# Forgetting attention: the mask products of two token blocks, one behind the other

## The chip, the cores and the metric

The kernel runs on one core of a Trainium2 chip. The metric is the device time of one launch in microseconds, the median over runs. The core has a matrix engine (TensorE, PE in the profile; its weight loads are the rows PEld), a vector engine (VectorE, DVE), a scalar engine (ScalarE, ACT), GpSimd (POOL) and SyncE (SP), which issues the DMAs. Each engine works through its own instructions in program order and waits for the others by semaphores.

## What is computed

A trunk of two decoder layers over 512 tokens of 1024 channels, in float32. Each layer is a SwiGLU half step, a token mixer and a second SwiGLU half step, with RMS norms around each. The mixer of the second layer is forgetting attention with 16 heads of 64 channels, and the change lies there:

```python
def _fox_attention(q, k, v, zf, b_f):
    logf = jax.nn.log_sigmoid(zf.astype(jnp.float32) + b_f.astype(jnp.float32))
    c = jnp.cumsum(logf.transpose(0, 2, 1), axis=-1)
    ...
        sc = jnp.einsum("bhqd,bhkd->bhqk", qs, kh).astype(jnp.float32) / math.sqrt(dh)
        sc = sc + cs[..., :, None] - c[..., None, :]
        sc = jnp.where(tpos[:, None] >= key_pos[None, :], sc, NEG)
        p = jax.nn.softmax(sc, axis=-1)
        return jnp.einsum("bhqk,bhkd->bhqd", p.astype(vh.dtype), vh)
```

## The kernel before

A float32 matrix product is made of three products of rounded parts (type float32r): each operand is split into a high part, rounded by ScalarE (`split`, line 69), and a low part, the rest, by VectorE; `mm3` (lines 74 to 76) adds high x high, high x low and low x high in one PSUM bank. The tile framework places the instructions: it takes the program, and with a timing model of its own it puts each engine's instructions into an order. So code that stands together is not together on an engine unless the data or a declared dependency makes it so.

`odd` (from line 599) is the mixer of the second layer. Per head, `project` computes the queries and keys (24 products of 512 columns), and `put_qk` empties that bank into four tiles QA, KA, QC, KC (lines 620 to 627), of which there are two sets, for even and odd heads. `project_v` computes the values of four heads for one block of 128 tokens (24 products of 256 columns).

`scores(h)` is where the change lies. The 512 query tokens of a head are four blocks b of 128, and block b sees (b + 1) x 128 keys. Its scores are a sum of three products in PSUM: line 688 (QA and KA, which also carry the gates), line 689 (the low parts), and line 690, the mask: a bf16 identity times a bf16 triangle of zeros and -1e30, added to the last 128 columns of the block. Then VectorE takes the maximum over the keys (692), ScalarE the exponential and its sum (693), VectorE the reciprocal (694) and the scaling (695). The scores of a head take three of four PSUM banks of the pool `acc`: blocks 0 and 1 share one, block 2 and block 3 have one each. A product into a bank waits until the exponentials that read it are done.

`transposed` turns the probabilities, ten blocks of 128 x 128 a head (line 710), into banks of the pool `mm`, and splits them; `values` multiplies them with the values (line 720, eight products). The loop calls scores(h + 1) ahead of transposed(h), so that a head's softmax runs beside the projections and the values of the head before. Heads are counted from 0.

Of the kernel before, what the change touches and what calls it, by code (L numbers as in the profile page):

```python
# [7 lines left out]


# [2 lines left out]

# [9 lines left out]
AF = mybir.ActivationFunctionType  # L22
ALU = mybir.AluOpType
AX = mybir.AxisListType
PSUM = bass.MemoryType.PSUM

P = 128
S = 512
NT = S // P
# [11 lines left out]
class Kernel:  # L41
# [145 lines left out]
    def turn_half(self, t, h, xg, which):  # L187
        nc = self.nc
        tp = self.psum(which)
        for k in range(4):  # L190
            nc.tensor.transpose(tp[:, k * P : (k + 1) * P], xg[:, k * P : (k + 1) * P], self.ident)
        ks, toks = slice(4 * h, 4 * h + 4), slice(t * P, (t + 1) * P)
        self.turned = self.split(self.hT[0][:, ks, toks], self.hT[1][:, ks, toks],
                                 tp.rearrange("p (k c) -> p k c", c=P))


    def ffn(self, l, s, norms, nxt, held=None):
# [401 lines left out]
    def odd(self, l, i, nxt):  # L599
        nc, tc, a = self.nc, self.tc, self.a  # L600
        w_qk, w_v0, w_v, w_out = (a["fox_w_" + n][i] for n in ("qk", "v0", "v", "out"))
        H = 16
        with ExitStack() as ctx:
# [10 lines left out]
            QA, KA, QC, KC = ([pc.tile([P, S], F32R, name=f"{n}{m}") for m in range(2)]  # L614
                              for n in ("qa", "ka", "qc", "kc"))
# [60 lines left out]
            def scores(h):  # L676
                m = h % 2
                banks = [self.psum("acc") for _ in range(3)]
                outs = [banks[0][:, 0:P], banks[0][:, P : 3 * P], banks[1][:, : 3 * P], banks[2]]
                pes = [self.wk() for _ in range(3)]  # L680
                pr = [pes[0][:, 0:P], pes[0][:, P : 3 * P], pes[1][:, : 3 * P], pes[2]]
                nm = self.small.tile([P, NT], F32, name="fnm")
                sm = self.small.tile([P, NT], F32, name="fsm")
                for b in range(NT):
                    n = (b + 1) * P
                    toks = slice(b * P, n)
                    ps = outs[b]
                    nc.tensor.matmul(ps, QA[m][:, toks], KA[m][:, :n], start=True, stop=False)  # L688
                    nc.tensor.matmul(ps, QC[m][:, toks], KC[m][:, :n], start=False, stop=False)
                    nc.tensor.matmul(ps[:, b * P : n], self.ident16, self.tri, start=False, stop=True)  # L690
                    bs = slice(b, b + 1)
                    nc.vector.tensor_reduce(nm[:, bs], ps, AX.X, ALU.max, negate=True)
                    nc.scalar.activation(pr[b], ps, AF.Exp, bias=nm[:, bs], accum_out=sm[:, bs])
                    nc.vector.reciprocal(sm[:, bs], sm[:, bs])
                    nc.vector.tensor_scalar(pr[b], pr[b], sm[:, bs], None, ALU.mult)
                return pr

            half = {}
# [63 lines left out]
            for h, (o, u) in enumerate(zip(pqk, u01)):  # L762
                self.proj(o[:, 256:], u, slice(256, 512))
                put_qk(h, o)
            project_v(1, 0)
            pr = scores(0)
            for h in range(H):
                pr2 = scores(h + 1) if h + 1 < H else None
                if h == 0:
                    project(h + 2)  # L770
                at = transposed(pr)
                if 0 < h < H - 2:
                    project(h + 2)
                if h >= 12:
                    early(h - 12)
                elif h >= 4:
                    project_v(h // 4 + 1, h % 4)
                elif h < 3:
                    project_v(1, 1 + h)
                values(h, at)  # L780
                pr = pr2
# [6 lines left out]
            for t in range(NT):  # L788
                toks = slice(t * P, (t + 1) * P)
# [160 lines left out]
```

## Time and profile before

| | us |
|---|---|
| median of 3 runs | 1948.91 (1948.52 to 1951.02) |
| the profiled execution | 1946.51 |
| its span | 1944.7 |
| TensorE busy in the span | 1911.6 |
| mask products (line 690), 64 of them, busy | 14.7 |

The span runs from the first to the last instruction of one profiled execution; the launch around it makes the difference to its time. Busy time of TensorE counts overlapping products once. [...] Attention of the second layer lies between 1340 and 1580 us.

### The profile page before, as it was taken

The page shows a single profiled execution, that of the slowest core. Times are in us where ns is not written, and L with a number is a line of the kernel's source. Part 1 is how long each engine was busy: PE and PEld are TensorE (multiplying, and loading weights), DVE is VectorE, ACT ScalarE, POOL GpSimd, SP SyncE. Part 2 cuts the span into 40 slices and gives each one's busy share as a digit, 9 for nine tenths or more (in the row PEclk, how much of TensorE's full clock was granted, in tenths as well). Part 3 has the DMA queues.
Part 4 walks back from the last instruction along what each step waited for, and adds up shares of the span by engine and source line. Part 5 has one row for each costly group of instructions (what it writes and reads, how often), then busy time and mean ns, then how long its engine had stood idle before and what let it go on. Part 6 is the DMA issues. An engine that isn't in the chain of part 4 may idle for free.

```text
span 1944.7 us, 24019 instructions
## 1 busy us (share of the span) xinstructions
PE 1911.6 (98%) x9715; PEld 1624.2 (84%) x9715; DVE 941.9 (48%) x1355; ACT 722.9 (37%) x1245; POOL 187.3 (10%) x250
## 2 busy tenths in 40 slices
PE   9999999999999999999999999999999999999998
PEld 8888888988788888888988888898888888888887
DVE  6333333589764333343633333356667563333333
ACT  6322221435654222222532222246666553222221
POOL 1000000333230000000200000014331110000000
PEclk9999999999999999999999999999999999999999
DMA  6323232131024323221442323222121323232311
GB/s 205 121 88 107 87 130 76 44 100 65 22 98 152 103 92 100 96 98 33 142 130 87 107 88 102 73 67 66 66 65 56 109 86 123 93 101 90 106 55 44
DMA packets 51265, 178.39 MB, mean 92 GB/s; under 512 B 7346, under 2 KB 7346, under 8 KB 51154
## 3 DMA queue, kind: packets, MB, share of 16 engines
q1 hardware_dynamic: 51154, 176.86, 28.1%
q8 instruction: 76, 1.25, 0.3%
q14 instruction: 35, 0.29, 0.1%
HBM read 174.74 MB, written 2.10 MB: 91 GB/s over the span
## 4 chain that ended last, share of the span: by engine, by line
PE 52%; issue 39%; DVE 3%; ACT 3%; POOL 2%; DMA 1%; POOLq 0%; DVEq 0%; SPq 0%; ACTq 0%
PE mm L74 14%; PE mm L75 14%; PE mm L76 14%; PE acc L74 2%; PE acc L75 2%; PE acc L76 2%; PE mm L710 1%; ACT whi L69 1%; POOL rstd L136 1%; PE mm L720 1%; POOL ms L134 1%; DMA raw<-in_ffn_w_up_dram 1%; ACT junk L141 1%; PE acc L688 0%; POOL wlo L69 0%
## 5 line engine op out<-in xcount | busy, mean ns | idle before, releaser
L74 PE MATMUL mm<-hhi,whi 128*128 128x512 f32 (+1 forms) x1952 | 693.6, 357 | 8.4 <-ACT hhi L69 7.8
L75 PE MATMUL mm<-hlo,whi 128*128 128x512 f32 (+1 forms) x1952 | 695.6, 357 | 2.7 <-DVE hlo L69 2.4
L76 PE MATMUL mm<-hhi,wlo 128*128 128x512 f32 (+1 forms) x1952 | 695.4, 357 | 0.0
L69 ACT CAST whi<-raw 128x1024 fp32r<-128x1024 f32 x319 | 331.3, 1050 | 894.7 <-issue 259.9
L69 DVE TENSOR_TENSOR wlo<-raw,whi 128x1024 fp32r<-128x1024 f32 (+1 forms) x293 | 355.0, 1226 | 370.3 <-ACT whi L69 355.9
L74 PEld LDWEIGHTS mm<-hhi,whi 128*128 128x128 f32 x1952 | 368.0, 189 | 62.9 <-ACT hhi L69 9.7
L75 PEld LDWEIGHTS mm<-hlo,whi 128*128 128x128 f32 x1952 | 369.6, 189 | 56.0 <-DVE hlo L69 4.1
L76 PEld LDWEIGHTS mm<-hhi,wlo 128*128 128x128 f32 x1952 | 369.6, 189 | 52.3
L215 DVE TENSOR_TENSOR wk<-mm,wk 128x512 f32<-128x512 f32 (+1 forms) x96 | 62.1, 647 | 291.6 <-PE mm L76 246.2
L252 DVE TENSOR_TENSOR ysb<-mm,ysb 128x512 f32<-128x512 f32 x128 | 88.5, 691 | 161.4 <-PE mm L76 161.4
L134 POOL TENSOR_SCALAR ms<-ss 128x1 f32<-128x1 f32 x48 | 24.0, 501 | 1463.1 <-ACT junk L141 1461.6
L76 PE MATMUL mm<-whi,alo 128*128 128x512 f32 x352 | 137.1, 389 | 0.0
L75 PE MATMUL mm<-wlo,ahi 128*128 128x512 f32 x352 | 137.0, 389 | 0.0
L76 PE MATMUL acc<-whi,alo 128*128 128x512 f32 x352 | 136.9, 389 | 0.0
L74 PE MATMUL acc<-whi,ahi 128*128 128x512 f32 x352 | 136.9, 389 | 0.0
L75 PE MATMUL acc<-wlo,ahi 128*128 128x512 f32 x352 | 136.9, 389 | 0.0
L74 PE MATMUL mm<-whi,ahi 128*128 128x512 f32 x352 | 136.8, 390 | 0.0
L214 ACT ACTIVATE wk<-mm 128x512 f32<-128x512 f32 (+1 forms) x96 | 53.0, 552 | 69.7 <-PE mm L76 69.7
L76 PEld LDWEIGHTS mm<-whi,alo 128*128 128x128 f32 x352 | 66.1, 188 | 13.8
L75 PEld LDWEIGHTS acc<-wlo,ahi 128*128 128x128 f32 x352 | 66.1, 188 | 13.8
L76 PEld LDWEIGHTS acc<-whi,alo 128*128 128x128 f32 x352 | 66.1, 188 | 13.7
L74 PEld LDWEIGHTS acc<-whi,ahi 128*128 128x128 f32 x352 | 66.0, 188 | 13.8
(213 smaller groups left out, 1962.0 us busy)
## 6 DMA issues: line engine op xcount, KB each, us to landing
raw<-in_ffn_w_gate_dram SPq DMA_DIRECT2D x88, 512.0 KB, 3.4
raw<-in_ffn_w_up_dram SPq DMA_DIRECT2D x88, 512.0 KB, 3.7
raw<-in_ffn_w_down_dram SPq DMA_DIRECT2D x88, 512.0 KB, 3.4
raw<-in_fox_w_qk_dram SPq DMA_DIRECT2D x16, 512.0 KB, 3.5
raw<-in_ab_w_in_dram SPq DMA_DIRECT2D x14, 512.0 KB, 3.4
raw<-in_ab_w_out_dram SPq DMA_DIRECT2D x8, 512.0 KB, 3.4
raw<-in_fox_w_out_dram SPq DMA_DIRECT2D x8, 512.0 KB, 3.5
gpost<-in_norm_g_dram SPq DMA_DIRECT2D x6, 512.0 KB, 3.8
```

What stands on the lines that cost most here:

```text
L69: return nc.scalar.copy(hi, src), (eng or nc.vector).tensor_tensor(lo, src, hi.bitcast(F32), ALU.subtract)
L74: mm(out, a[0], b[0], start=start, stop=False)
L75: mm(out, a[0], b[1], start=False, stop=False)
L76: return mm(out, a[1], b[0], start=False, stop=stop)
L134: nc.gpsimd.tensor_scalar(ms, ss[:, 0:1], ss[:, 1:2], eps, ALU.add, ALU.add)
L136: nc.gpsimd.tensor_tensor(r, ms, self.mhalf, ALU.pow)
L141: return self.nc.scalar.activation(junk, src, AF.Square, scale=scale, accum_out=out)
L214: nc.scalar.activation(sg, pg, AF.Silu)
L215: nc.vector.tensor_tensor(av, pu, sg, ALU.mult)
L252: nc.vector.tensor_tensor(ysb[t], p, ysb[t], ALU.add)
L710: nc.tensor.transpose(pt[:, c0 : c0 + P], pr[b][:, kb * P : (kb + 1) * P], self.ident)
L720: nc.tensor.matmul(po[:, kb * P :], vv, at[kb][n], start=kb == 0 and n == 0, stop=kb == NT - 1 and n == 1)
```

## The change

In `scores`, the blocks are computed in two pairs, (0, 2) and (1, 3), whose banks differ within a pair. Of a pair, lines 688 and 689 of both blocks come first, and then the two mask products. A new helper declares, for each TensorE instruction of a pair, that it comes after the one before it; it adds an order on the engine and no semaphore. Softmax is as before, block by block in the order of the pairs. No instruction is added or removed. The changed lines 700, 701 and 703 answer to 688, 689 and 690 of before; 706 to 709 to 692 to 695; 724 to 710; 734 to 720.

```diff
+    @contextmanager
+    def in_order(self, engine):
+
+        traced = self.nc.cur_bb.bb.instructions
+        first = len(traced)
+        yield
+        own = [i for i in traced[first:] if i.engine == engine.engine]
+        for before, i in zip(own, own[1:]):
+            self.tc.add_manual_dep(i, before.name, mybir.DependencyInfo(
+                mybir.DependencyClass.NoSync, mybir.DependencyReason.DATA), reason="in_order")
...
-                for b in range(NT):
-                    n = (b + 1) * P
-                    toks = slice(b * P, n)
-                    ps = outs[b]
-                    nc.tensor.matmul(ps, QA[m][:, toks], KA[m][:, :n], start=True, stop=False)
-                    nc.tensor.matmul(ps, QC[m][:, toks], KC[m][:, :n], start=False, stop=False)
-                    nc.tensor.matmul(ps[:, b * P : n], self.ident16, self.tri, start=False, stop=True)
-                    bs = slice(b, b + 1)
-                    nc.vector.tensor_reduce(nm[:, bs], ps, AX.X, ALU.max, negate=True)
...
+                for bb in ((0, 2), (1, 3)):
+                    with self.in_order(nc.tensor):
+                        for b in bb:
+                            ps, n, toks = outs[b], (b + 1) * P, slice(b * P, (b + 1) * P)
+                            nc.tensor.matmul(ps, QA[m][:, toks], KA[m][:, :n], start=True, stop=False)
+                            nc.tensor.matmul(ps, QC[m][:, toks], KC[m][:, :n], start=False, stop=False)
+                        for b in bb:
+                            nc.tensor.matmul(outs[b][:, b * P :], self.ident16, self.tri, start=False, stop=True)
+                    for b in bb:
+                        ps, bs = outs[b], slice(b, b + 1)
+                        nc.vector.tensor_reduce(nm[:, bs], ps, AX.X, ALU.max, negate=True)
...
```

The order of the instructions changes on TensorE, VectorE, ScalarE and GpSimd within this stage and nowhere else; SyncE's is the same. Three places on TensorE follow, before and with the change. A mask product is a weight load and a product there, since the bf16 load is an instruction of its own; the float32 products carry theirs.

The scores of head 3, as most heads have them, before (`ka`, `qa`, `kc`, `qc` are the tiles of `put_qk`, 128x384 is block 2, 128x512 block 3):

```order
L710 MATMUL mm<-ident,wk 128x128 x4
L688 MATMUL acc<-ka_10106,qa_10104 128x128
L688 MATMUL acc<-ka_10106,qa_10104 128x384
L688 MATMUL acc<-ka_10106,qa_10104 128x512
L689 MATMUL acc<-kc_10110,qc_10108 128x128
L690 LDWEIGHTS ident_172
L690 MATMUL acc<-tri,ident_172 128x128
L689 MATMUL acc<-kc_10110,qc_10108 128x384
L690 LDWEIGHTS ident_172
L690 MATMUL acc<-tri,ident_172 128x128
L689 MATMUL acc<-kc_10110,qc_10108 128x512
```

and with the change:

```order
L724 MATMUL mm<-ident,wk 128x128 x3
L700 MATMUL acc<-ka_10106,qa_10104 128x128
L701 MATMUL acc<-kc_10110,qc_10108 128x128
L700 MATMUL acc<-ka_10106,qa_10104 128x384
L701 MATMUL acc<-kc_10110,qc_10108 128x384
L703 LDWEIGHTS ident_172
L703 MATMUL acc<-tri,ident_172 128x128
L703 LDWEIGHTS ident_172
L703 MATMUL acc<-tri,ident_172 128x128
L724 MATMUL mm<-ident,wk 128x128 x7
```

Block 3 has gone from this place to the pair (1, 3), which stands 26 projection products and seven transposes later.

The first scores of the stage, before, from block 2 of head 0 to block 1 of head 0 (`qa_10103` is of the even heads, `qa_10104` of the odd ones):

```order
L688 MATMUL acc<-ka_10105,qa_10103 128x384
L689 MATMUL acc<-kc_10109,qc_10107 128x384
L690 LDWEIGHTS ident_172
L690 MATMUL acc<-tri,ident_172 128x128
L688 MATMUL acc<-ka_10105,qa_10103 128x512
L689 MATMUL acc<-kc_10109,qc_10107 128x512
L690 LDWEIGHTS ident_172
L690 MATMUL acc<-tri,ident_172 128x128
L688 MATMUL acc<-ka_10106,qa_10104 128x128
L689 MATMUL acc<-kc_10110,qc_10108 128x128
L690 LDWEIGHTS ident_172
L690 MATMUL acc<-tri,ident_172 128x128
```

and with the change, from the masks of its pair (0, 2) on:

```order
L703 LDWEIGHTS ident_172
L703 MATMUL acc<-tri,ident_172 128x128
L703 LDWEIGHTS ident_172
L703 MATMUL acc<-tri,ident_172 128x128
L700 MATMUL acc<-ka_10105,qa_10103 128x256
L701 MATMUL acc<-kc_10109,qc_10107 128x256
L700 MATMUL acc<-ka_10105,qa_10103 128x512
L701 MATMUL acc<-kc_10109,qc_10107 128x512
```

Block 1 (128x256) now comes ahead of block 3 and of head 1's block 0; before, it came behind both.

The last head (15), before, from its block 1 to the transposes (the rows of line 720 are the values of head 14):

```order
L720 MATMUL mm<-pThi_12502,vv_11742 128x512
L688 MATMUL acc<-ka_10106,qa_10104 128x256
L689 MATMUL acc<-kc_10110,qc_10108 128x256
L690 LDWEIGHTS ident_172
L690 MATMUL acc<-tri,ident_172 128x128
L720 MATMUL mm<-pTlo_12503,vv_11742 128x512
L720 MATMUL mm<-pThi_12511,vv_11882 128x384
L720 MATMUL mm<-pTlo_12512,vv_11882 128x384
L720 MATMUL mm<-pThi_12519,vv_12023 128x256
L720 MATMUL mm<-pTlo_12520,vv_12023 128x256
```

and with the change:

```order
L734 MATMUL mm<-pThi_12511,vv_11882 128x384
L700 MATMUL acc<-ka_10106,qa_10104 128x256
L701 MATMUL acc<-kc_10110,qc_10108 128x256
L700 MATMUL acc<-ka_10106,qa_10104 128x512
L701 MATMUL acc<-kc_10110,qc_10108 128x512
L703 LDWEIGHTS ident_172
L703 MATMUL acc<-tri,ident_172 128x128
L703 LDWEIGHTS ident_172
L703 MATMUL acc<-tri,ident_172 128x128
L734 MATMUL mm<-pTlo_12512,vv_11882 128x384
L734 MATMUL mm<-pThi_12519,vv_12023 128x256
```

Two products of the values of 512 and 384 columns have gone ahead of the pair, and block 3 has come in. In both kernels ten transposes stand behind the values, the four that read block 3 last in the change.

## Rows read from the trace of the kernel before

**Rows 1.** The page: busy time per engine, and the chain that ended last.
```profile
PE 1911.6 (98%) x9715; PEld 1624.2 (84%) x9715; DVE 941.9 (48%) x1355; ACT 722.9 (37%) x1245; POOL 187.3 (10%) x250
PE 52%; issue 39%; DVE 3%; ACT 3%; POOL 2%; DMA 1%; POOLq 0%; DVEq 0%; SPq 0%; ACTq 0%
```

**Rows 2.** Windows: stretch, us; busy time by engine; clock, DMA share, GB/s.
```profile
1350.00:1360.00 10.00, 9.47 (x61) 8.77 (x62) 6.13 (x15) 4.18 (x11) 0.16 (x1) 0.83 0.01 2
1340.00:1580.00 240.00, 227.62 (x1327) 195.74 (x1326) 159.91 (x350) 145.62 (x325) 60.76 (x57) 0.99 0.21 66
```

**Rows 3.** Weight loads of lines 690 and 689, 1340 to 1580 us: ns min/median/max.
```profile
L690 PEld LDWEIGHTS <-ident x64: 95/96/99, 1340.8 to 1529.6; 128*128 128x128 bf16 x64
L689 PEld LDWEIGHTS acc<-kc,qc x64: 186/192/201, 1340.6 to 1529.4; 128*128 128x128 f32 x64
```

**Rows 4.** Timeline of PE: start us, duration us, instruction; head 1's values, head 3's scores.
```profile
1368.38 0.40 PE L720 MATMUL mm<-pTlo,vv 128*128 128x512 f32 x1
1368.61 0.33 PE L720 MATMUL mm<-pThi,vv 128*128 128x384 f32 x1
1368.79 0.34 PE L720 MATMUL mm<-pTlo,vv 128*128 128x384 f32 x1
...
1369.20 0.22 PE L720 MATMUL mm<-pThi,vv 128*128 128x128 f32 x1
1369.26 0.28 PE L720 MATMUL mm<-pTlo,vv 128*128 128x128 f32 x1
1369.37 0.62 PE L710 MATMUL mm<-ident,wk 128*128 128x128 f32 x4
1369.75 0.77 PE L688 MATMUL acc<-ka,qa 128*128 128x128 f32 x3
1370.36 0.22 PE L689 MATMUL acc<-kc,qc 128*128 128x128 f32 x1
1370.43 0.23 PE L690 MATMUL acc<-tri,ident 128*128 128x128 bf16 x1
1370.46 0.42 PE L689 MATMUL acc<-kc,qc 128*128 128x384 f32 x1
1370.73 0.23 PE L690 MATMUL acc<-tri,ident 128*128 128x128 bf16 x1
```

**Rows 5.** Waits of PE, 1340 to 1351.5: us in total, times, longest.
```profile
PE acc L688 <- ACT wk L693: 3.1, 4, 1.1
PE acc L688 <- issue: 0.3, 1, 0.3
```

**Rows 6.** Timeline of PE at the end of that stretch.
```profile
1349.98 1.94 PE L710 MATMUL mm<-ident,wk 128*128 128x128 f32 x9
1351.57 0.56 PE L74 MATMUL mm<-whi,hhi 128*128 128x256 f32 x1
```

**Rows 7.** Waits of PE, 1351.5 to 1580.
```profile
PE acc L688 <- ACT wk L693: 1.6, 3, 0.8
PE mm L710 <- DVE wk L695: 1.6, 3, 0.7
PE mm L710 <- DVE kc L624: 1.5, 1, 1.5
```

**Rows 8.** Timeline of PE: the last head's mask product, transposes and what follows.
```profile
1529.64 0.23 PE L690 MATMUL acc<-tri,ident 128*128 128x128 bf16 x1
1531.57 1.20 PE L710 MATMUL mm<-ident,wk 128*128 128x128 f32 x9 [0.53 <-DVE wk L695]
1532.53 0.48 PE L74 MATMUL mm<-whi,chi 128*128 128x512 f32 x1
```

**Rows 9.** Groups by form, 1340 to 1580: busy us, mean ns, idle before.
```profile
L692 DVE TENSOR_REDUCE fnm<-acc 128x1 f32<-128x512 f32 x16 | 10.9, 679 | 0.1
L693 ACT ACTIVATE wk<-acc,fnm 128x512 f32<-128x512 f32 x16 | 11.2, 699 | 1.5 <-DVE fnm L692 1.4
L693 ACT ACTIVATE wk<-acc,fnm 128x256 f32<-128x256 f32 x16 | 7.6, 478 | 18.6 <-DVE fnm L692 18.5
```

More of the change, by code (lines that the diff above doesn't have):

```diff
@@ L10 @@
 import math
-from contextlib import ExitStack
+from contextlib import ExitStack, contextmanager
 import concourse.bass as bass
@@ L683, in scores @@
                 sm = self.small.tile([P, NT], F32, name="fsm")
-                for b in range(NT):
-                    n = (b + 1) * P
-                    toks = slice(b * P, n)
-                    ps = outs[b]
-                    nc.tensor.matmul(ps, QA[m][:, toks], KA[m][:, :n], start=True, stop=False)
-                    nc.tensor.matmul(ps, QC[m][:, toks], KC[m][:, :n], start=False, stop=False)
-                    nc.tensor.matmul(ps[:, b * P : n], self.ident16, self.tri, start=False, stop=True)
-                    bs = slice(b, b + 1)
-                    nc.vector.tensor_reduce(nm[:, bs], ps, AX.X, ALU.max, negate=True)
-                    nc.scalar.activation(pr[b], ps, AF.Exp, bias=nm[:, bs], accum_out=sm[:, bs])
-                    nc.vector.reciprocal(sm[:, bs], sm[:, bs])
-                    nc.vector.tensor_scalar(pr[b], pr[b], sm[:, bs], None, ALU.mult)
+                for bb in ((0, 2), (1, 3)):
[9 more added lines that the diff above has]
+                        nc.vector.tensor_reduce(nm[:, bs], ps, AX.X, ALU.max, negate=True)
+                        nc.scalar.activation(pr[b], ps, AF.Exp, bias=nm[:, bs], accum_out=sm[:, bs])
+                        nc.vector.reciprocal(sm[:, bs], sm[:, bs])
+                        nc.vector.tensor_scalar(pr[b], pr[b], sm[:, bs], None, ALU.mult)
                 return pr
```

## The prediction

> **What bounds the kernel now.** I read the page first. TensorE is busy 98% of the span, and the chain that ended last is TensorE work and its issue, 91% together [rows 1]: whatever TensorE issues or waits for is time. The windows then give the attention stage that the change touches, 1340 to 1580 us: TensorE busy 227.6 of 240 us, VectorE 160, ScalarE 146 [rows 2]. So about 12 us there are waits, and the rest is TensorE's own pace. Then comes the timeline of one head, for what a product costs in sequence; the waits, for what its neighbours hold back; and the order of the changed kernel, for what now stands where. The profiled execution took 1946.51 us, its span 1944.7. The median of the runs is 2.4 us above it, so I work out a difference against the profile and take it from the median.
>
> **What a mask product costs.** Starts of plain float32 products follow each other by 0.23 us (512 columns), 0.18 (384) and 0.06 (128) [rows 4]. From the first mask product of head 3 to the next, with one 384-column product between, starts lie 0.30 us apart [rows 4]: 0.12 above the plain 0.18. By the ends (start plus duration) the mask adds 0.08 after the float32 product, and the float32 product after it takes 0.22 for 0.18. I split the 0.12 as 0.07 for the mask and 0.05 for what follows. The weight loads suggest why: a float32 load lasts 192 ns, a bf16 one 96 [rows 3], so a float32 product behind a short one finds its weights not yet there. If so, it is shortness that costs, not the type. The row that bears this out has no bf16 in it: lines 688 of blocks 0, 2 and 3 end 0.53 us after the transposes end, for plain slots of 0.06, 0.18 and 0.23, together 0.47 [rows 4]. The 384 columns behind the 128 pay 0.06 too. I call this an exposure.
>
> **The change part by part.** *Pairs.* The order shows all 64 mask products in 32 pairs, and nothing inside a pair. A head pays five exposures now: behind line 688 of block 0, and behind each of four masks (line 689 of block 0 is followed by a mask, whose load is light). With the change it pays four: behind lines 688 and 689 of block 0, which now stand ahead of float32 products, and behind two pairs. So one exposure of 0.05 goes, not two, and each second mask changes from 0.07 to an unknown x. No bf16 product follows another in this trace. Bounds for x: 0.05, under the shortest slot, if nothing waits; 0.11, a 128-column slot plus an exposure, if the second load is not hidden. I take 0.06, the 128-column slot, since its load lasts half as long as a float32 one. A head then saves 0.05 + 2 x 0.01 = 0.07, sixteen heads 1.1 us: **-1.1 us** (-1.5 at x = 0.05, +0.5 at 0.11).
>
> [...]
>
> *The first two heads.* There TensorE waits 3.4 us in 1340 to 1351.5, nearly all for exponentials to free score banks [rows 5]. Now block 3 of head 0 and block 0 of head 1 fill the time until block 0's exponential is done; with the pair (1, 3) in order they stand behind block 1, and that wait grows from 1.1 [rows 5] to about 2. On the other hand four of ten transposes and lines 688 of head 2's blocks 2 and 3, some 0.9 us, leave the stretch ahead of the projection. I book waits at 0, with 0.8 either way. Behind them the clock fell: it shows 0.83 over 1350 to 1360 [rows 2], which is 1.7 us of clock lost. There nine transposes took 1.59 us to the next product [rows 6], against 0.96 in the last head [rows 8]. Waits that come earlier let it fall earlier, while TensorE waits anyway; I book **-0.6** (between -1.7 with no fall and +1.7 with a second).
>
> *The last head.* Now its block 1 alone is late: mask start to transposes 1.93 us, and to the next product 2.89 [rows 8]. In the change block 3 comes with block 1, and its four transposes last. Behind block 1 its reduction adds 0.68 on VectorE, and its exponential is 0.22 longer than block 1's (699 against 478 ns) [rows 9]: 1.93 + 0.68 + 0.22 = 2.83, plus four transposes of 0.11 (0.96 / 9) is 3.27. In between TensorE has less to do: 512 and 384 columns of values (0.41) went ahead of the pair, and a second mask (0.06) came in. Wait now 0.7 (2.89 less about 2.2 of work), then 1.4: **+0.7** (0.3 to 1.3).
>
> *The heads between.* After 1351.5 block 1 waits 1.6 us for exponentials in three places, transposes 1.6 for scaled probabilities (0.53 of it in the last head [rows 8]), and once 1.5 for VectorE to empty a projection's bank [rows 7]. Block 1 now stands behind 17 or more projection products in most heads and right behind five transposes in two (heads 11 and 13): -0.5. Pairs (1, 3) come late in heads 4, 5 and 10, with 4 to 6 projection products and the values before the next transposes; block 3's probabilities then arrive later: +0.4. In ScalarE's order the 0.70 us exponential of head 4's block 3 [rows 9] now stands ahead of emptying the projection's bank, so the 1.5 us wait grows by it: +0.7. Together **+0.6** (-1.0 to +2.5). VectorE and ScalarE work otherwise only in another order, hidden by TensorE as far as they have slack, a third of the stage; the GpSimd order moves with them, the DMA issues not at all.
>
> Sum: -1.1 - 0.6 + 0.7 + 0.6 = **-0.4 us**: 1946.1 against the profile, 1948.5 against the median. About 0.2% (3.9 us) is what a measurement of this kernel tells from no change.
>
> **The rivals.** *Faster:* the cost lies in the change of type. Then the 128-column float32 products expose nothing, pairs halve the turns, and a head saves 2 x (0.05 + 0.01) = 0.12, 1.9 us in all. With no fall of the clock (-1.7) and the waits of the heads between mostly gone (-0.7) that is -4.3: 1944.6. For it: the single fall comes behind waits that the change reshapes. Against it: the exposure without bf16 [rows 4].
>
> *Slower:* block 3 becomes the late one. In order, its scores wait for block 1's bank, its softmax of 2.8 us starts late, and transposes wait for it. If its chain is lengthened by other work on VectorE and ScalarE by as much as the longest such wait now, 1.5 us [rows 7], heads 4, 5 and 10 pay 4.5, the last one 1.3, less 1.1: +4.7, 1953.6. It decides where the transposes wait over 1 us for line 709 of block 3 in three heads or more. For it: it is the widest block, 679 and 699 ns [rows 9]. Against it: in the order most pairs (1, 3) have 20 or more projection products and the values behind them, over 3 us.
>
> *The pair buys nothing:* x is 0.11, the second load as exposed as a float32 one. The products lose 0.5 where they gained 1.1: 1950.1. For it: no row shows two such loads in a row. Against it: the bf16 load lasts half as long [rows 3].
>
> **How the numbers follow.** The forecast gets 0.62, faster 0.17, slower 0.13, nothing bought 0.08. A quarter of the faster case and a fifth of the slower stay within 0.2%, the forecast and the last rival wholly. That gives faster 0.13, same 0.77, slower 0.10. The range reaches down to the faster rival, 1944.6, and up 3.3 us from the forecast, 1951.8, which takes in x at its upper bound and a second fall of the clock; the full slower case is left out.
>
> **What would show it.** In the changed profile: mask products in pairs, the second about 0.06 behind the first, the product after the pair still about 0.05 late, and the 384-column product behind line 701 of block 0 late too; the stage shorter by some 1 us of busy time; a wait of about 2 us ahead of line 700 with 256 columns near 1343; one fall of the clock there; a longer wait of line 724 in the last head and before head 4's last transposes. A second mask at 0.11, transposes waiting over 1 us in several heads, or no fall at all would make the forecast wrong, each in the way of its rival.

## The result, and the profile after

The change takes 1962.18 us (median of 4 runs, 1961.0 to 1964.23), the kernel before beside it 1949.81 (4 runs, 1948.52 to 1951.02): the ratio is 1.0065 (95% interval 1.0053 to 1.0078), 12.4 us slower. The forecast was no change (1948.5), its range ended at 1951.8.

The page of the changed kernel: busy time per engine, and the chain that ended last, to be read beside [rows 1].

```profile
PE 1921.0 (98%) x9715; PEld 1629.1 (83%) x9715; DVE 949.8 (48%) x1355; ACT 722.1 (37%) x1245; POOL 187.5 (10%) x250
PE 52%; issue 39%; DVE 4%; ACT 3%; POOL 2%; DMA 1%; POOLq 0%; DVEq 0%; SPq 0%; ACTq 0%
```

The page hardly shows where the time went: TensorE's busy time rises by 9.4 us with the same 9715 instructions, VectorE's by 7.9, and its share of the chain from 3% to 4%. The profiled execution of the change took 1962.77 us with a span of 1961.0, 16.3 more than that of before, so I first ask which stage they fall into. From the first score product to the last product of the values the stage lasts from 1340.6 to 1538.7 before, from 1343.4 to 1554.8 after. The windows of the change over that stage, over four short stretches in it, and over a stretch long before it (columns as in [rows 2]):

```profile
1343.40:1554.80 211.40, 195.98 (x1133) 164.83 (x1132) 141.80 (x314) 124.14 (x278) 45.67 (x38) 0.97 0.16 53
...
1346.20:1349.60 3.40, 3.29 (x13) 2.33 (x13) 2.19 (x6) 2.52 (x8) 1.92 (x3) 0.50 0.44 133
1353.00:1356.40 3.40, 3.40 (x17) 3.40 (x18) 2.89 (x9) 1.34 (x4) 0.00 (x0) 0.51 0.00 0
1390.60:1394.00 3.40, 3.40 (x10) 2.64 (x9) 1.81 (x7) 0.96 (x4) 0.00 (x0) 0.50 0.24 96
1404.20:1407.60 3.40, 3.38 (x8) 2.71 (x9) 2.21 (x4) 1.05 (x2) 0.00 (x0) 0.51 0.15 63
...
500.00:560.00 60.00, 57.19 (x244) 45.34 (x244) 36.56 (x58) 34.66 (x72) 12.56 (x12) 0.91 0.20 74
```

The same windows of the kernel before:

```profile
1340.60:1538.70 198.10, 189.75 (x1132) 163.12 (x1131) 134.76 (x314) 124.31 (x278) 45.56 (x38) 0.99 0.18 56
...
1350.30:1353.70 3.40, 3.40 (x19) 3.40 (x17) 2.45 (x7) 1.55 (x3) 0.00 (x0) 0.50 0.00 0
...
500.00:560.00 60.00, 57.19 (x258) 45.43 (x257) 37.88 (x60) 37.34 (x79) 13.46 (x14) 0.97 0.23 79
```

The stage grew by 13.3 us. Its idle time on TensorE (length less busy) went from 8.4 to 15.4, 7.1 more. Its busy time grew by 6.2, and most of that is the clock: four stretches of 3.4 us at half clock (0.50 and 0.51 granted) where there was one, so three more, in each of which 1.7 us of work is lost: 5.1, an estimate from these lengths and clocks. About 1 us of busy time stays without a name.

The other 2.8 us lie before the stage, where the order of the instructions is the same: over 500 to 560 the clock shows 0.91 against 0.97, and fewer products get done (244 against 258) in the same 57.19 us of busy time. That isn't the change's doing (last section), and it is why the profiles differ by more than the medians. Over whole runs the granted clock has a mean of 0.992 in the change's four and 0.9946 in 29 of the kernel before: times some 1950 us that is 15.7 and 10.6 us lost. So by this estimate about 5 of the 12.4 us are clock, and 7.4 are time in which TensorE waits or is busy longer.

The waits of TensorE in the change, 1340 to 1600 us:

```profile
PE mm L724 <- DVE wk L709: 7.5, 9, 1.9
PE acc L700 <- ACT wk L707: 4.3, 3, 2.0
...
PE mm L74 <- DVE wk L743: 1.7, 4, 0.7
PE mm L724 <- DVE kc L635: 1.0, 1, 1.0
```

Transposes waited 1.6 us in three places for VectorE's scaling of the probabilities (line 695) [rows 7]; now they wait 7.5 in nine for the same instruction (line 709). Waits for score banks are no longer than they were (4.3 against 3.1 and 1.6 [rows 5, 7]). So the question is why the scaling comes late. The timeline of the change, all engines, around the three longest of these waits:

```profile
1383.83 4.76 POOL L69 TENSOR_TENSOR wlo<-raw,whi 128x1024 fp32r<-128x1024 f32 x2 [0.81 <-DVE fnm L706]
...
1386.82 2.05 DVE L709 TENSOR_SCALAR wk<-wk,fsm 128x512 f32<-128x512 f32 x1
...
1388.93 0.66 PE L724 MATMUL mm<-ident,wk 128*128 128x128 f32 x4 [1.64 <-DVE wk L709]
...
1399.40 2.35 POOL L69 TENSOR_TENSOR wlo<-raw,whi 128x1024 fp32r<-128x1024 f32 x1 [1.82 <-ACT whi L69]
...
1400.17 1.86 DVE L709 TENSOR_SCALAR wk<-wk,fsm 128x512 f32<-128x512 f32 x1
...
1402.09 0.44 PE L724 MATMUL mm<-ident,wk 128*128 128x128 f32 x2 [1.89 <-DVE wk L709]
...
1507.48 2.65 DVE L709 TENSOR_SCALAR wk<-wk,fsm 128x512 f32<-128x512 f32 x1
1507.49 2.36 POOL L69 TENSOR_TENSOR wlo<-raw,whi 128x1024 fp32r<-128x1024 f32 x1 [1.19 <-ACT whi L69]
...
1510.19 1.00 PE L724 MATMUL mm<-ident,wk 128*128 128x128 f32 x5 [1.17 <-DVE wk L709]
```

In each, VectorE scales block 3 while GpSimd subtracts the rounded part of a projection's weight (`wlo`, the split that `project` gives to GpSimd). The scaling, 0.48 us elsewhere, takes 2.05, 1.86 and 2.65, and each time it ends 0.28 us after GpSimd's instruction does (1386.82 + 2.05 = 1388.87 against 1383.83 + 4.76 = 1388.59). GpSimd's is no longer than elsewhere (2.35, 2.35 and 2.36, against a median of 2.40 for the 16 from 1330 to 1600 us). So in these three places the scaling lasts until GpSimd's instruction is done; what holds it up, no trace shows. In the first two GpSimd's instruction began earlier, by about 0.6 (the second of the two in the row of 4.76, which begins in its middle) and by 0.77 us; in the third the recorded starts are 0.01 apart.

With 0.48 in place of 2.05, 1.86 and 2.65 us, and everything else in its place, these three waits (4.7 us in all) would come down to 0.1, 0.5 and 0: an estimate from these rows. A block of 256 columns meets GpSimd too, just before the first of them (1385.14 us, 1.24 us long where the 16 of this width had a mean of 0.36 before), and transposes wait 0.55 us for it.

The traces also show that little margin was left (the program tells which transposes read block 3). From the end of block 3's scaling to the first transpose that reads it there is a median of 6.5 us before and of 0.5 in the change; it is under 1 us in one head of 16 before, and in ten of them now. So block 3 has become late in most heads, and in the three where its scaling is also stretched TensorE stands.

Before, the weight split met a scaling once in the stage, on a block of 128 columns (timeline of before), and no transpose stood long for it (the longest wait for a scaling is 0.7 us [rows 7]):

```profile
1401.75 2.41 POOL L69 TENSOR_TENSOR wlo<-raw,whi 128x1024 fp32r<-128x1024 f32 x1 [7.10 <-ACT whi L69]
...
1402.26 1.97 DVE L695 TENSOR_SCALAR wk<-wk,fsm 128x128 f32<-128x128 f32 x1
```

The groups by form say it in one row each; first before, then the change (mean ns is the last number but one):

```profile
L695 DVE TENSOR_SCALAR wk<-wk,fsm 128x512 f32<-128x512 f32 x16 | 7.6, 477 | 0.0
```

```profile
L709 DVE TENSOR_SCALAR wk<-wk,fsm 128x512 f32<-128x512 f32 x16 | 12.8, 798 | 0.2
```

### The profile page after: what moved, and what is told of

It is laid out like the page before. It is cut to its first block, busy times and chain, and to the rows that moved or that the text cites. A ratio compares the mean times of both kernels' runs of the same rounds, so it can differ in the third digit from the quotient of the medians.

```text
span 1961.0 us, 24002 instructions
## 1 busy us (share of the span) xinstructions
PE 1921.0 (98%) x9715; PEld 1629.1 (83%) x9715; DVE 949.8 (48%) x1355; ACT 722.1 (37%) x1245; POOL 187.5 (10%) x250
## 4 chain that ended last, share of the span: by engine, by line
PE 52%; issue 39%; DVE 4%; ACT 3%; POOL 2%; DMA 1%; POOLq 0%; DVEq 0%; SPq 0%; ACTq 0%
PE mm L74 15%; PE mm L75 14%; PE mm L76 14%; PE acc L74 2%; PE acc L75 2%; PE acc L76 2%; ACT whi L69 1%; POOL rstd L136 1%; POOL ms L134 1%; DVE wlo L69 1%; ACT junk L141 1%; PE mm L724 1%; PE mm L734 0%; DVE wk L709 0%; PE acc L700 0%
## 5 line engine op out<-in xcount | busy, mean ns | idle before, releaser
L74 PE MATMUL mm<-hhi,whi 128*128 128x512 f32 (+1 forms) x1952 | 696.2, 359 | 10.6 <-ACT hhi L69 7.7
```

Source lines behind the costliest of these rows:

```text
L74: mm(out, a[0], b[0], start=start, stop=False)
```

## The experiments

**Theory:** the declared pair (1, 3) puts block 3's softmax behind block 1's. Its scaling then falls beside GpSimd's weight split and is stretched, the transposes wait, and the clock falls behind the waits. **Rivals:** the pair (1, 3) is late by its order alone, without GpSimd; the waits for score banks, above all in the first two heads, and the fall behind them cost the time; the products of a pair cost more than a product alone. All times are medians, compared with runs of the kernel before on the same chip (29, 25 and 22 of them for the three groups of runs; medians 1949.80, 1950.17 and 1950.25).

**The declared order taken out.** The code stays in pairs, the scheduler is free.

```diff
-                    with self.in_order(nc.tensor):
+                    with ExitStack():
```

> The changed kernel without the declared order: blocks still written as pairs (0, 2), (1, 3), but the framework may place them. In its order only the masks of blocks 0 and 2 stand together (16 pairs, not 32), block 3 follows at once and block 1 alone is late, as before. Theory A (the loss comes from block 3 being tied behind block 1, so its softmax is late): within 2 us of before, about 1949. Theory B (A, but the price is mostly VectorE's scaling of the late block colliding with GpSimd's weight split): the same, about 1949, and no scaling above 1 us beyond the one that before has. Rival C (any new order of this stage loses as much, by luck and by falls of the clock): 1954 or more.

Measured: 1950.45 us, ratio 0.9998 (0.9988 to 1.0007). The order that comes out keeps the blocks 0 and 2 of all 16 heads as pairs and puts block 3 early again. Transposes wait 1.5 us for the scaling, as before. So the loss is in what the declaration forces on top, which is above all the pair (1, 3).

**One pair alone declared.** First the pair (0, 2), then the pair (1, 3), the rest free.

```diff
-                for bb in ((0, 2), (1, 3)):
+                for bb in ((0, 2), (3,), (1,)):
```

> Only blocks 0 and 2 paired, in declared order; blocks 3 and 1 by themselves, each with its mask right behind. Theory A (block 3 tied behind block 1 makes the loss): within 3 us of before, 1949 to 1953; what is left over before is block 1's wait for block 0's exponential, since block 0's mask now stands behind block 2's products. Rival D (the declared order of any group is what costs): 1955 or more.

```diff
-                for bb in ((0, 2), (1, 3)):
+                for bb in ((0,), (2,), (1, 3)):
```

> The other half: blocks 0 and 2 each with its own mask, blocks 1 and 3 paired in declared order, so block 3 is late as in the change. A: most of the loss is here, 1957 to 1963, with the transposes waiting 5 us or more for line 709. If first and late pair each brought half (D): 1954 to 1957 here and about the same for the first pair alone.

Measured: 1950.70, ratio 1.0002 (0.9993 to 1.0012), with the pair (0, 2); 1960.84, ratio 1.0055 (1.0038 to 1.0072), with the pair (1, 3). The second one's waits of TensorE, 1340 to 1560:

```profile
PE mm L724 <- DVE wk L709: 7.8, 8, 1.9
PE acc L700 <- ACT wk L707: 4.5, 2, 2.5
```

Its scalings of block 3 are as long as the change's (group by form of the same kernel):

```profile
L709 DVE TENSOR_SCALAR wk<-wk,fsm 128x512 f32<-128x512 f32 x16 | 13.2, 825 | 0.3
```

The pair (1, 3) carries the loss within the intervals, and 16 mask pairs (0, 2) cost and gain nothing that can be measured. That speaks against the products of a pair as the cause; the pair's own products are read below, in the rows of head 3.

**GpSimd taken out of the way.** The projection's split goes to VectorE, whose own subtraction of the same tile lasts 1.23 us.

```diff
-                self.proj(out, self.unit(w_qk[h], P, eng=nc.gpsimd))
+                self.proj(out, self.unit(w_qk[h], P))
```

> The changed kernel with the low part of the query and key weights computed on VectorE instead of GpSimd (14 splits of 1024 columns, about 1.2 us each on VectorE, 2.4 on GpSimd). B: no scaling above 0.8 us, the transposes' waits for it fall from 7.5 to under 3 us, and the time comes back to 1950 to 1955. A without B: the late block still costs, and VectorE has 17 us more work: 1960 or more.

The same edit in the kernel before:

> Control for the run with the weight splits on VectorE: the same edit in the kernel before. If taking GpSimd out helps only where block 3 is late (B), this is within 2 us of before, 1948 to 1952, as before has one blocked scaling of 2 us and VectorE gets 17 us more work. If GpSimd's splits cost the kernel before as much too, it is 1945 or less.

Measured: 1953.39, ratio 1.0017 (1.0007 to 1.0026), in the change; 1948.64, ratio 0.9992 (0.9982 to 1.0002), in the kernel before. The group by form and the window of the stage, of the change with this edit:

```profile
L709 DVE TENSOR_SCALAR wk<-wk,fsm 128x512 f32<-128x512 f32 x16 | 7.7, 481 | 0.1
```

```profile
1340.00:1555.00 215.00, 202.45 (x1197) 171.68 (x1196) 152.26 (x334) 131.68 (x290) 32.34 (x32) 1.00 0.21 68
```

Two of its waits of TensorE, 1340 to 1560:

```profile
PE acc L700 <- ACT wk L707: 6.2, 5, 1.8
PE mm L724 <- DVE wk L709: 1.6, 3, 0.9
```

No scaling takes over 0.49 us, transposes wait 1.6 us for it in three places, as before, and the clock does not fall in the stage in this profile. Of 12.4 us 3.6 are left.

The edit also changes VectorE's list, and with it the order on TensorE: the pair (1, 3) of head 4, for one, comes earlier. That could give back time by itself. But block 3 is as late as in the change: from the end of its scaling to the first transpose that reads it there is a median of 0.75 us (0.5 in the change), and it is under 1 us in ten heads, as in the change. So a late block 3 without the collision makes TensorE wait no longer for the scaling than before. This, and the nothing that the same edit does to the kernel before, is the strongest evidence for the theory.

Not all of what comes back is that wait. In the stage (1345.4 to 1545.6 us here) TensorE is idle for 12.2 us, against 15.4 in the change and 8.4 before: other waits grew. The rest of the difference between the two profiles is busy time, most of it clock. Over the runs the mean granted clock is 0.9942 here, 0.9946 in the kernel before and 0.992 in the change. Waits of 1.6 to 1.8 us stand in this profile without a fall behind them: that it is the waits for the scaling that make the clock fall is not shown.

**Block 3 scaled by ScalarE.** It keeps the split on GpSimd and takes away the instruction that meets it.

```diff
-                        nc.vector.tensor_scalar(pr[b], pr[b], sm[:, bs], None, ALU.mult)
+                        if b == 3:
+                            nc.scalar.mul(pr[b], pr[b], sm[:, bs])
+                        else:
+                            nc.vector.tensor_scalar(pr[b], pr[b], sm[:, bs], None, ALU.mult)
```

> The changed kernel with block 3's probabilities scaled on ScalarE instead of VectorE. GpSimd keeps its weight splits, and both pairs stay. Theory B (a good part of the loss is the scaling of the late, wide block blocked by GpSimd's split): no VectorE scaling above 1.3 us except of narrower blocks, waits of the transposes 3 to 5 us less, and 3 to 8 us faster than the change, 1954 to 1959. If the lateness alone costs (A without B): within 2 us of the change, 1960 or more.

Measured: 1956.13, ratio 1.0026 (1.0016 to 1.0035): 6.0 us over before, half of the loss gone. ScalarE takes 723 ns for what VectorE does in 477, and waits remain (a row of the group, and the waits, 1340 to 1560; lines 712 and 727 answer to 709 and 724):

```profile
L710 ACT ACTIVATE wk<-wk,fsm 128x512 f32<-128x512 f32 x16 | 11.6, 723 | 5.6 <-DVE fsm L708 5.6
```

```profile
PE acc L700 <- ACT wk L707: 5.0, 3, 2.1
PE mm L727 <- DVE wk L712: 2.9, 3, 1.5
PE mm L727 <- ACT wk L710: 2.3, 2, 1.6
PE mm L727 <- DVE kc L635: 1.5, 1, 1.5
```

So a second way around the collision also gives back time, less of it; the scaling itself got longer, on an engine that has the exponentials. This edit too changed the order on TensorE, and here block 3 is less late than in the change (under 1 us ahead of its transposes in seven heads, not ten), so it separates the two less cleanly.

**The first two heads left alone.** No pairs there, to see what the early waits and the fall behind them are worth.

```diff
-                for bb in ((0, 2), (1, 3)):
+                for bb in ((0, 2), (1, 3)) if h > 1 else ((0,), (1,), (2,), (3,)):
```

> The changed kernel with pairs from head 2 on only; heads 0 and 1 as before, so the first scores wait for exponentials as before (3.4 us there, not 4 or more), and from head 5 on the order is the change's. Theory A and B (late block 3 and the blocked scaling in the heads between): most of the loss stays, 1956 to 1961. Rival E (the longer waits of the first heads and the falls of the clock behind them carry the loss): 1953 or less.

Measured: 1957.81, ratio 1.0038 (1.0025 to 1.0051). Waits for score banks fall to 2.4 us, those for the scaling stay at 7.1 in eight places. Some 60% of the loss (7.6 of 12.4 us) is made behind the first heads; the rest may be theirs. In this profile the clock falls for 6.8 us at 1351.5 although heads 0 and 1 are as before, so a fall there needs no pairs.

**Other groups.** Three masks in a row, with block 3 early, and then the late pair turned around:

```diff
-                for bb in ((0, 2), (1, 3)):
+                for bb in ((0, 2, 3), (1,)):
```

> Masks in groups (0, 2, 3) and (1) with declared order: as many exposures saved as by the pairs, but block 3 no longer tied to block 1. A and B: 1.1 to 1.5 us faster than before in TensorE's products, 1947 to 1949 in all. Rival D (the declared order itself costs, since TensorE is held at one instruction of a group): slower than before by 3 us or more, with waits of lines 700 and 724 over 9 us in the stage.

Measured: 1957.27, ratio 1.0035 (1.0025 to 1.0046), which the theory of the late block did not give; the waits are those that its rival, the waits for score banks, named. The waits, 1340 to 1560, and a timeline of TensorE:

```profile
PE acc L700 <- ACT wk L707: 8.0, 8, 1.8
PE mm L724 <- DVE kc L635: 2.1, 2, 1.5
PE mm L724 <- DVE wk L709: 1.9, 3, 0.9
```

```profile
1475.91 0.34 PE L703 MATMUL acc<-tri,ident 128*128 128x128 bf16 x3
...
1478.06 0.39 PE L700 MATMUL acc<-ka,qa 128*128 128x256 f32 x1 [1.80 <-ACT wk L707]
```

Here transposes don't wait, and block 1 does: block 0's mask now stands behind the products of three blocks, its exponential is late, and block 1 shares its bank. It is another price of tying blocks together, which the change itself pays mostly in its first two heads (waits of 2.03 and 1.52 us, below).

```diff
-                for bb in ((0, 2), (1, 3)):
+                for bb in ((0, 2), (3, 1)):
```

> Pairs (0, 2) and (3, 1): block 3's two float32 products go early, but its mask still waits for block 1's, so its softmax stays late while TensorE is not held ahead of its products. A and B: still slow, 5 to 12 us over before, with waits of the transposes for the scaling (line 709) of 5 us or more. If the loss came from TensorE standing behind block 1's wait in the first heads (rival D): most of it gone, within 3 us of before.

Measured: 1952.65, ratio 1.0019 (1.0008 to 1.0029), single runs from 1950.0 to 1958.8. Transposes wait 3.0 us for the scaling in four places. With block 3 first in the late pair three quarters of the loss go. Block 3 is less late here: its scaling ends a median of 3.5 us ahead of the first transpose that reads it, not 0.5, and none of its scalings takes over 0.7 us. That fits a cost that hangs on the place of block 3's softmax among VectorE's instructions, and doesn't tell lateness from collision. The 5 to 12 us of loss that the theories of a late pair gave were not reached.

**GpSimd taken out where the order is not the late one.**

> A candidate against both kernels: masks of blocks 0 and 2 together where the framework puts them, block 3 early, and the query and key weight splits on VectorE. The two parts by themselves gave 0.9998 and 0.9992 of before. If they add and the second is real: 1947 to 1949, ratio 0.9985 to 0.9995. If both are noise: within 0.05% of before.

> A second candidate, the first pair in declared order with the splits on VectorE: the same as the other candidate within 2 us, 1947 to 1950, with no scaling above 0.8 us and transposes waiting under 2 us for line 709.

Measured: without a declared order 1955.27, ratio 1.0027 (1.0017 to 1.0037), a miss; with the pair (0, 2) alone 1949.64, ratio 0.9996 (0.9987 to 1.0004). In the first the scheduler, given VectorE's longer list, put block 1 right behind six transposes in three heads, where it waits 1.47 us each time for its bank; with two waits in the first heads (the longest 1.9) that is 6.8 us in five places. So an edit that only moves a split can cost 5 us, and the order that comes out is the likely reason (its profile was the fastest of ten runs, 4.7 us under the median, so it shows no more than a part). The times of all these kernels may carry a few us of such placement. The 3.6 us left in the change without GpSimd may be of that kind: TensorE is idle 3.9 us longer in its stage than before (12.2 against 8.4), 1.5 of it at score banks (6.2 against 4.7 [rows 5, 7]). No version is measurably faster than the kernel before.

| kernel | us over before | mean scaling of block 3, ns |
|---|---|---|
| the change | 12.4 | 798 |
| pair (1, 3) alone | 10.7 | 825 |
| change, heads 0 and 1 free | 7.6 | 700 |
| groups (0, 2, 3), (1) | 7.5 | 478 |
| no declared order, split on VectorE | 5.0 | 480 |
| change, split on VectorE | 3.6 | 481 |
| pairs (0, 2), (3, 1) | 2.9 | 519 |
| no declared order | 0.7 | 477 |
| pair (0, 2) alone | 0.5 | 481 |
| pair (0, 2) alone, split on VectorE | -0.6 | 480 |

The three largest losses are those with stretched scalings of block 3. They aren't the only way to lose: two kernels lose 7.5 and 5.0 us with none, and wait 8.0 and 6.8 us for score banks.

The clock goes much the same way. From 1360 us to the end of the stage it falls to 0.5 in six of the 13 profiles, one of each kernel: for 6.8, 6.8 and 13.6 us in the three kernels with stretched scalings of block 3, and for 6.8, 3.4 and 3.4 in the groups (0, 2, 3), the pairs (0, 2), (3, 1) and the free order with the split on VectorE. All six are slower than the kernel before; the other seven, two of which are slower too, show no fall there.

## Why the prediction was wrong

**What held.** The masks: two stand behind each other, and the rows of head 3 (timeline of TensorE in the change) give the prices that I took.

```profile
1372.88 0.27 PE L701 MATMUL acc<-kc,qc 128*128 128x128 f32 x1
1372.99 0.39 PE L700 MATMUL acc<-ka,qa 128*128 128x384 f32 x1
1373.21 0.33 PE L701 MATMUL acc<-kc,qc 128*128 128x384 f32 x1
1373.39 0.28 PE L703 MATMUL acc<-tri,ident 128*128 128x128 bf16 x2
```

A single mask lasts 0.23 us, the two together 0.28, so x is 0.05 to 0.06, and the rival in which it is 0.11 falls. The 384 columns behind the 128 of line 701 end 0.23 after them (1373.38 against 1373.15), 0.05 over the plain 0.18: the exposure is where I put it, behind a short product, not behind a type. But the 1.1 us that this should save doesn't show in the stage's busy time.

**The first heads.** The waits ahead of the two block 1's there (timeline of TensorE in the change) are

```profile
1346.31 0.58 PE L700 MATMUL acc<-ka,qa 128*128 128x256 f32 x1 [2.03 <-ACT wk L707]
...
1351.25 0.38 PE L700 MATMUL acc<-ka,qa 128*128 128x256 f32 x1 [1.52 <-ACT wk L707]
```

and so as booked: the first 2.03 where I expected about 2, together 3.55 against 3.4, and 0.41 more ahead of head 0's transposes. The clock term had the wrong sign in this profile: instead of falling earlier and less it fell twice (1346.2 and 1353.0 in the windows above), +1.7, the upper bound that I gave and did not take. That is not all the pairs' doing: with heads 0 and 1 as before the clock fell for as long there (6.8 us). That waits let the clock fall was my estimate; no run shows it.

**The last head.** From its first mask to the next projection product:

```profile
1544.86 0.28 PE L703 MATMUL acc<-tri,ident 128*128 128x128 bf16 x2
...
1546.79 0.77 PE L724 MATMUL mm<-ident,wk 128*128 128x128 f32 x5 [0.88 <-DVE wk L709]
1547.74 0.66 PE L724 MATMUL mm<-ident,wk 128*128 128x128 f32 x4 [0.18 <-DVE wk L709]
1548.34 0.50 PE L74 MATMUL mm<-whi,chi 128*128 128x512 f32 x1
```

That is 3.48 us for a forecast of 3.27. The term was the wait: 1.85 us of it were booked as work, so 1.6 are wait where 0.7 were, +0.9; by the profile's own gaps it is 1.06 against 0.53 [rows 8], +0.5. The term of +0.7 lies between and was right.

**The heads between: here it failed.** The step was "VectorE and ScalarE work otherwise only in another order, hidden by TensorE as far as they have slack", with the GpSimd order that "moves with them" at no price. I gave each instruction the duration that it had before, 0.48 us for a scaling. In the new order three of block 3's scalings meet GpSimd and take four to five and a half times that. The waits for the scaling between the first heads and the last one went from 1.0 to 6.0 us; the other waits of that stretch grew by 0.7. Two more falls of the clock come behind the waits at 1389 and 1402, +3.4. So the term of +0.6, with an upper bound of +2.5, is about +9 in this profile, 5 of it waits for the scaling.

The other half of the step is the margin. I held against the slower rival that most pairs (1, 3) have over 3 us of TensorE's work behind them, beside a softmax of 2.8 us. From block 3's second product to the end of its scaling it takes 3.1 us in the last head alone; over the 16 heads the median is 5.5 us, collisions or not (5.6 with the split on VectorE). With that the margin is gone in most heads.

**The slower rival** had the place right, transposes waiting for line 709 of block 3, and its condition was met: waits of 1.64, 1.89 and 1.17 us, in heads 3, 4 and 12, of which it had named head 4. It had half of the reason: block 3's chain is longer by other work, which takes the margin, but what makes the transposes wait is a scaling of 0.48 us that takes 1.86 to 2.65 beside GpSimd's subtraction. Its price, +4.7, came out at a bit over a third, and it gave the clock nothing. It got 0.13.

**Left open.** About 1 us of busy time in the stage beside the 1.1 that the pairs should have saved; what stretches the scaling beside GpSimd's subtraction; what makes the clock fall, and whether its part would be paid at the same waits each time; and what of the 3.6 us that stay without GpSimd is the lateness of block 3 and what is the order that this edit brought.

## What to carry to other kernels

The order declared on TensorE here changed the order on VectorE, ScalarE and GpSimd too, and in the new one a scaling of 0.48 us took up to 2.65 beside a subtraction on GpSimd. So look in the new order for the late block's VectorE instructions beside GpSimd's long ones, and don't carry durations over from the old order. Before tying two blocks together, ask which of them has the least time to its consumer; tying the pair whose banks were free early cost nothing, tying the late one 10.7 us. A saving of 0.07 us a head is small against where the scheduler then puts a block of work, so read the waits first and the products after.

## What the runs showed of the hardware that I had not expected

A 128x512 scaling of 0.48 us lasted up to 2.65 beside a GpSimd subtraction of 2.36, and ended 0.28 after it in three places of three. Narrower blocks that met the same subtraction for most of its length ended 0.21 after it (384 columns, with the pair (1, 3) alone), 0.15 (256, without a declared order) and 0.08 (128, in the kernel before). The subtraction was no longer for it (2.35, 2.35 and 2.36 us in the change's three, where the median is 2.40).

The clock differs between executions where the order of the instructions doesn't. In 76 runs of the kernel before the mean granted clock of a run lies between 0.991 and 0.997. Over 500 to 560 us, ahead of everything that these kernels change, TensorE is busy 57.18 to 57.20 us in each of the 13 profiles, and the clock of that stretch is 0.91 in six of them, 0.97 in five and 1.00 in two, with some 244, 258 and 264 products in it. One of the last, of the change with block 3 on ScalarE, beside the rows of the same stretch in the first section:

```profile
500.00:560.00 60.00, 57.20 (x263) 45.51 (x263) 39.45 (x62) 38.38 (x82) 14.50 (x16) 1.00 0.23 79
```

Over the runs of the kernel before, the longer ones are those with the lower mean clock (a correlation of -0.5 to -0.8 on the three chips). So a part of the run-to-run spread of some 5 to 9 us goes with the clock, and a fall of the clock in one profile is not by itself the work of a change.
